# A streaming encoder kernel whose expert tiles are requested at another point of the program, with its gates read in six pieces

## The chip, the cores and the metric

The kernel runs on one core of a Trainium2 chip. The time is device microseconds of one execution, from the first to the last thing that the core does. Three executions of the kernel before took 3267.62, 3263.42 and 3265.85 us, a median of 3265.85 us. A separate execution was profiled.

## The reference

The program computes two residual layers and a final RMSNorm for 512 tokens of width 1024. A layer is a mixer (attention and pooling in the even layer, attention and a recurrence in the odd one) and then a PEER expert block, in which each token picks 8 x 16 of 16384 single-neuron experts. Only the expert block is touched by the change:

```python
def peer_ffn(h, w_query, sub_k1, sub_k2, expert_u, expert_v):
    q = (xt @ w_query).reshape(n_tok, PEER_HEADS, 2, PEER_DKEY // 2)
    s1 = jnp.einsum('thd,nd->thn', q[:, :, 0], sub_k1)
    s2 = jnp.einsum('thd,nd->thn', q[:, :, 1], sub_k2)
    v1, i1 = lax.top_k(s1, PEER_TOPK)
    v2, i2 = lax.top_k(s2, PEER_TOPK)
    ...
    top_s, pos = lax.top_k(cand.astype(jnp.float32), PEER_TOPK)
    idx = jnp.take_along_axis(cand_idx, pos, axis=-1)
    gate = jax.nn.softmax(top_s, axis=-1)
    ...
        u = expert_u[ib]
        act = jax.nn.gelu(jnp.einsum('thkd,td->thk', u, xb), approximate=False)
        ve = expert_v[ib]
        return jnp.einsum('thk,thkd->td', (gb * act).astype(ve.dtype), ve)
```

## The kernel before, in words

The expert block (function `peer`, called once per layer) splits the tokens. For the first 384 tokens it computes all 16384 experts densely, as 128 blocks of 128 experts: block j needs a u tile (512 KB), whose product with the tokens goes through a GELU and gives the activations of the block, and a v tile (512 KB), whose product with the activations times the gates is added up in six banks of PSUM. The last 128 tokens are done sparsely: 256 row fetches of 512 KB (`row`, issued by GpSimd, five buffers) are reduced by VectorE.

Every fp32 operand is split into a high and a low part and each product is three matmuls (`mm3`, lines 182 to 184, for u; line 1680 for v). ScalarE makes the high part (line 151), VectorE the low part (`ul` at line 1355, `vl` and `Hl` at line 176). A raw tile's buffer comes free when its low part is made.

The order of the work is the order of the code, engine by engine. Each engine runs its instructions in turn, and so does the queue of SyncE (SP), which issues nearly all loads: a DMA that has to wait for its buffer holds back all DMAs behind it on SP.

The dense part has these stages in each layer:

1. The u stage. Blocks 0 to 52 are multiplied by u (`u_step`), while VectorE works out which experts each token picked and makes the gates as one-hot products. The gates of 16 tokens at a time are written to DRAM by ScalarE's queue (`gd<-gs`, 1 MB each, 24 of them). Activations of blocks 0 to 12 stay in SBUF (`act`, NB_ACT = 13 buffers); those of blocks 13 to 52 (NB_SPILL = 40) are written to DRAM from a tile with two buffers (`acts`, `ad<-acts`).
2. The first 40 steps of the v loop. Step j splits v tile j + 1 (`v_load`), reads one spilled activation tile back (`a_load`), makes the gated activations of block j + 1 (`h_make`: `Hf`, `Hh`, `Hl`) and issues the 18 matmuls of block j (`v_mm`). From step 4 on VectorE also takes about 0.85 row per step (`g_work`).
3. Steps 40 to 114, in which each step also does the 24 matmuls of one of the 75 blocks left for u, and about 2.9 rows.
4. Steps 115 to 125 with v alone, the last two blocks token group by token group, and the output.

The gates of a group of 8 blocks are read back from DRAM as one DMA of 1536 KB in runs of 512 bytes (`g_load`, line 1633, tile `gt` with two buffers). A v tile (`vr`, three buffers) is requested in `v_fetch` (line 1642), called at the head of `v_load`; a u tile (`ur`, three buffers) in `u_fetch` (line 1340).

```python
            def v_load(j):
                if j < TAIL:
                    v_fetch(j + 1)
                g_load(j + 3)
                r = VR.pop(j)
...
            for j in range(TAIL):
                v_load(j + 1)
                if j < NB_SPILL:
                    a_load(NB_ACT + j)
                ...
                h_make(j + 1)
                v_mm(j)
```

Of the kernel before, what the change touches and what calls it, by code (L numbers as in the profile page):

```python
# [13 lines left out]
F32 = mybir.dt.float32  # L14
F32R = mybir.dt.float32r
# [10 lines left out]
P = 128  # L26
# [1266 lines left out]
TD = 384  # L1293
# [3 lines left out]
GB = 16  # L1297
GJ = 8
G_STEP = 4.2
NB_ACT = 13  # L1300
NB_SPILL = 40
ROWS = 5
# [5 lines left out]
def peer(k, layer):  # L1308
    nc, tc = k.nc, k.tc
    I = k.I  # L1310
    with ExitStack() as st:
# [30 lines left out]
        def u_load(j):  # L1342
            if j < NE:
                u_fetch(j)
                u_fetch(j + 1)
                r = U[j]
                h = up.tile([P, KD, P], F32R, name="uh", bufs=4)
                k.act(h, r, AF.Copy)
                U[j] = (h, r)
# [8 lines left out]
        def u_mm(j, spill=False):  # L1358
            h, l = U.pop(j)
            ps = psU.tile([P, T], F32, name="ups", tag="mm")  # L1360
            for d in range(KD):
                mm3(k, ps[:, :TD], (h[:, d, :], l[:, d, :]), (hh[:, d, :TD], hl[:, d, :TD]), d == 0, d == KD - 1)
            a = up.tile([P, TD], F32, name="acts") if spill else ap.tile([P, TD], F32, name="act")
            k.act(a, ps[:, :TD], AF.Gelu)
# [259 lines left out]
        with ExitStack() as st2:  # L1624
# [4 lines left out]

            def g_load(j):  # L1630
                if j < NE and j % GJ == 0:
                    g = vp.tile([P, TD // GB, GJ, GB], F32, name="gt")
                    nc.sync.dma_start(g, gd[:, :, j:j + GJ, :].rearrange("b p j t -> p b j t"))
                    GG[j // GJ] = g

            VR, fetched = {}, set()

            def v_fetch(j):
                if j < NE and j not in fetched:
                    fetched.add(j)  # L1640
                    VR[j] = vp.tile([P, D], F32, name="vr", bufs=3)
                    nc.sync.dma_start(VR[j], I["peer_vp"][layer, j])

            def v_load(j):
                if j < TAIL:
                    v_fetch(j + 1)
                g_load(j + 3)
                r = VR.pop(j)
# [3 lines left out]
                else:  # L1652
                    h = vp.tile([P, D], F32R, name="vh")
                    l = vp.tile([P, D], F32R, name="vl")
                split_act(k, h, l, r)
                VV[j] = (h, l)

            def h_make(j):
# [4 lines left out]
                if j == NE - 1:  # L1663

                    h, l = (up.tile([P, TD], F32R, name="acts") for _ in range(2))
                else:
# [121 lines left out]

            v_fetch(0)
            v_fetch(1)  # L1790
            g_load(0)
            v_load(0)
# [12 lines left out]
            for j in range(TAIL):  # L1805
# [9 lines left out]
                v_mm(j)  # L1815
                if j == TAIL - 5:
                    v_fetch(NE - 1)
                if j == TAIL - 4:
# [211 lines left out]
```

## Time and profile before

| | |
|---|---|
| median of three executions | 3265.85 us (3263.42 to 3267.62) |
| profiled execution | 3267.5 us |
| its span, first to last instruction | 3265.7 us (1.8 us lie around it) |
| TensorE busy | 3133.8 us, 96% of the span |
| VectorE busy | 2429.3 us, 74% |
| ScalarE busy | 1419.4 us, 43% |
| bytes moved by DMA | 792.67 MB, 243 GB/s on average |
| mean granted TensorE clock | 0.984 of full speed |

PE is TensorE's matmuls and PEld its weight loads, DVE is VectorE, ACT ScalarE, POOL GpSimd, SP SyncE; a q behind the name (SPq, ACTq) marks the engine's DMA issues. A matmul's duration in the trace includes time in which the next one already runs, so that a step's pace is read from the starts and not from the durations. A wait is put down to what came last. Times within the run are counted from the span's start. The u stage lies at about 405 to 675 us in layer 0 and 2105 to 2380 us in layer 1; the first 40 steps of the v loop run from 687 to 868 us and from 2389 to 2567 us.

### The profile page before, as it was taken

To read this page: it belongs to the slowest core of one execution; us is meant where nothing else is said; L and a number is where in the kernel's file an instruction comes from. 1 tells how busy PE (TensorE), PEld (TensorE's weight loads), DVE (VectorE), ACT (ScalarE), POOL (GpSimd) and SP (SyncE) were. 2 spreads that over 40 slices of the span, in tenths; PEclk is the share of its full clock that TensorE was granted. 3 is DMA by queue.
4 is the path that set the end of the run, shared out by engine and by line. 5 is a ranking of instruction groups with operands and counts; after the bars stand their busy time and mean duration, and the time that the engine had idled before them with its cause. 6 is when DMAs were issued, how large, how long until landed. Compare 5 with 4: busy or idle time off the path is not lost.

```text
span 3265.7 us, 55046 instructions
## 1 busy us (share of the span) xinstructions
PE 3133.8 (96%) x21696; PEld 2739.4 (84%) x21696; DVE 2429.3 (74%) x4725; ACT 1419.4 (43%) x1974; POOL 893.2 (27%) x696
## 2 busy tenths in 40 slices
PE   6998999999999999999999898999999999999998
PEld 5777899977799999997677787899977899999997
DVE  5246799957688888887666456899957788888886
ACT  3353367743333333333534534367733333333334
POOL 1004200023344444442220104100013344444442
PEclk8999999999999999999999999999999999999999
DMA  8523246799899999995621014256799999999984
GB/s 313 203 96 131 100 156 245 251 314 319 289 342 334 331 327 339 339 328 184 219 71 53 5 63 155 97 179 237 266 318 315 313 333 330 327 337 342 328 316 162
DMA packets 318276, 792.67 MB, mean 243 GB/s; under 512 B 23872, under 2 KB 159424, under 8 KB 305728
## 3 DMA queue, kind: packets, MB, share of 16 engines
q1 hardware_dynamic: 222992, 438.73, 38.8%
q0 software_dynamic: 75008, 274.78, 24.4%
q10 hardware_dynamic: 20016, 75.64, 6.1%
q8 instruction: 170, 2.79, 0.3%
q14 instruction: 90, 0.74, 0.1%
HBM read 714.57 MB, written 74.45 MB: 242 GB/s over the span
## 4 chain that ended last, share of the span: by engine, by line
PE 80%; DVE 9%; DMA 5%; ACT 4%; issue 3%; SPq 0%; ACTq 0%; DVEq 0%
PE o L1680 27%; PE ups L182 9%; PE ups L184 9%; PE ups L183 9%; PE bk L182 3%; PE bk L184 3%; PE bk L183 3%; DMA vr<-peer_vp 2%; PE bk L723 2%; PE qps L182 2%; PE gps L1568 2%; PE qps L183 2%; PE qps L184 2%; PE adaps L242 1%; DVE ul L1355 1%
## 5 line engine op out<-in xcount | busy, mean ns | idle before, releaser
L182 PE MATMUL ups<-phh,uh 128*128 128x384 f32 x2048 | 695.4, 340 | 6.6 <-ACT acts L151 6.6
L184 PE MATMUL ups<-phh,ul 128*128 128x384 f32 x2048 | 689.9, 337 | 0.0
L183 PE MATMUL ups<-phl,uh 128*128 128x384 f32 x2048 | 688.5, 336 | 0.0
L1702 POOL DMA_INDIRECT row<-peer_u,xres x256 | 344.5, 1346 | 1125.7 <-PE gps L1568 552.1
L151 ACT ACTIVATE vh<-vr 128x1024 fp32r<-128x1024 f32 x254 | 269.7, 1062 | 556.0 <-issue 454.0
L1680 PE MATMUL o<-vh,Hh 128*128 128x512 f32 x1524 | 477.9, 395 | 30.1 <-ACT Hh L151 30.1
L1680 PE MATMUL o<-vh,Hl 128*128 128x512 f32 x1524 | 474.5, 393 | 0.0
L1680 PE MATMUL o<-vl,Hh 128*128 128x512 f32 x1524 | 474.4, 393 | 0.0
L1702 POOL DMA_INDIRECT row<-peer_v,xres x256 | 337.4, 1318 | 428.2 <-DVE xres L1718 333.7
L176 DVE TENSOR_TENSOR vl<-vr,vh 128x1024 fp32r<-128x1024 f32 x254 | 311.0, 1224 | 131.4 <-ACT vh L151 129.9
L182 PEld LDWEIGHTS ups<-phh,uh 128*128 128x128 f32 x2048 | 387.1, 189 | 13.1 <-ACT acts L151 7.2
L183 PEld LDWEIGHTS ups<-phl,uh 128*128 128x128 f32 x2048 | 387.0, 189 | 5.8
L184 PEld LDWEIGHTS ups<-phh,ul 128*128 128x128 f32 x2048 | 386.5, 189 | 0.9 <-DVE ul L1355 0.6
L1680 PEld LDWEIGHTS o<-vh,Hh 128*128 128x128 f32 x1524 | 284.4, 189 | 86.6 <-ACT Hh L151 37.8
L1680 PEld LDWEIGHTS o<-vl,Hh 128*128 128x128 f32 x1524 | 288.2, 189 | 63.3
L1680 PEld LDWEIGHTS o<-vh,Hl 128*128 128x128 f32 x1524 | 288.0, 189 | 62.3
L1355 DVE TENSOR_TENSOR ul<-ur,uh 128x1024 fp32r<-128x1024 f32 x256 | 312.0, 1219 | 24.1 <-ACT uh L151 21.4
L1721 DVE SCALAR_TENSOR_TENSOR gacc<-row,xres,gacc 128x1024 f32<-128x1024 f32 x256 | 327.6, 1280 | 2.0 <-DMA row<-peer_v,xres 1.2
L176 DVE TENSOR_TENSOR Hl<-Hf,Hh 128x384 fp32r<-128x384 f32 x254 | 141.9, 559 | 241.4 <-ACT Hh L151 241.4
L1718 DVE SCALAR_TENSOR_TENSOR xres<-row,xres 128x1024 f32<-128x1024 f32 x256 | 311.8, 1218 | 0.6 <-DMA row<-peer_u,xres 0.6
L151 ACT ACTIVATE uh<-ur 128x1024 fp32r<-128x1024 f32 x256 | 269.6, 1053 | 22.3 <-DMA ur<-peer_uT 7.2
L151 ACT ACTIVATE act<-ups 128x384 f32<-128x384 f32 x176 | 86.5, 492 | 370.6 <-PE ups L184 370.5
(475 smaller groups left out, 4583.7 us busy)
## 6 DMA issues: line engine op xcount, KB each, us to landing
ur<-peer_uT SPq DMA_DIRECT2D x256, 512.0 KB, 5.8
vr<-peer_vp SPq DMA_DIRECT2D x256, 512.0 KB, 7.0
gt<-gd SPq DMA_DIRECT2D x32, 1536.0 KB, 15.5
adaw<-ada_w SPq DMA_DIRECT2D x32, 1024.0 KB, 7.0
wraw<-peer_wq SPq DMA_DIRECT2D x32, 512.0 KB, 3.4
ad<-acts ACTq DMA_DIRECT2D x80, 192.0 KB, 3.6
act<-ad SPq DMA_DIRECT2D x80, 192.0 KB, 5.0
wraw<-od_w_in SPq DMA_DIRECT2D x30, 512.0 KB, 3.6
```

The lines of the kernel that those rows point to most:

```text
L151: return self.nc.scalar.activation(out, in_, func, **kw)
L176: (eng or k.nc.vector).tensor_tensor(lo, src, hi.bitcast(F32), op=ALU.subtract)
L182: mm(out, w[0], x[0], start=start, stop=False, skip_group_check=True)
L183: mm(out, w[0], x[1], start=False, stop=False, skip_group_check=True)
L184: mm(out, w[1], x[0], start=False, stop=stop, skip_group_check=True)
L723: mm(ps[h, a, :], l(h, a), r(h, a), start=start and a == 0, stop=stop, skip_group_check=True)
L1355: nc.vector.tensor_tensor(l, r, h.bitcast(F32), op=ALU.subtract)
L1568: nc.tensor.matmul(ps[:, i, :], A[:, 2 * q + i // 2, :, i % 2], B[r][:, 2 * q + i // 2, :, i % 2], start=r == 0, stop=r == 1, skip_group_c ...
L1680: mm(O_[t][b], w[:, ts], v[:, 512 * b:512 * b + 512], start=s, stop=e, skip_group_check=True)
L1702: nc.gpsimd.indirect_dma_start(out=r, out_offset=None, in_=I[f"peer_{kind}{layer}"], in_offset=bass.IndirectOffsetOnAxis(ap=eidx[:, c:c + ...
L1718: nc.vector.scalar_tensor_tensor(junk, r, 1.0, htok, op0=ALU.mult, op1=ALU.mult, accum_out=dots[:, c:c + 1])
L1721: nc.vector.scalar_tensor_tensor(acc, r, wts[:, c:c + 1], acc, op0=ALU.mult, op1=ALU.add)
```

## The change

One activation buffer of 13 becomes a third buffer of the spilled activations, so that 12 blocks stay in SBUF and 41 are spilled; the sum of 53 is unchanged. `v_fetch` is called behind the split of a v tile and requests the tile that will take the buffer which that split frees, three blocks ahead; the order of the requests is a list, in which the last block's tile stands where it is used. `u_load` requests up to two blocks ahead in place of one. The gates of a group of 8 blocks are read by six DMAs of 256 KB (four blocks of 16 tokens each), one in each of the first six steps of the group before; the first group is still one DMA.

```diff
--- before.py
+++ after.py
@@ -1297,8 +1297,8 @@
 GB = 16
 GJ = 8
 G_STEP = 4.2
-NB_ACT = 13
-NB_SPILL = 40
+NB_ACT = 12
+NB_SPILL = 41
 ROWS = 5
 ADA_M = 12
 TAIL = NE - 2
@@ -1341,8 +1341,8 @@
 
         def u_load(j):
             if j < NE:
-                u_fetch(j)
-                u_fetch(j + 1)
+                for i in range(3):
+                    u_fetch(j + i)
                 r = U[j]
                 h = up.tile([P, KD, P], F32R, name="uh", bufs=4)
                 k.act(h, r, AF.Copy)
@@ -1360,7 +1360,7 @@
             ps = psU.tile([P, T], F32, name="ups", tag="mm")
             for d in range(KD):
                 mm3(k, ps[:, :TD], (h[:, d, :], l[:, d, :]), (hh[:, d, :TD], hl[:, d, :TD]), d == 0, d == KD - 1)
-            a = up.tile([P, TD], F32, name="acts") if spill else ap.tile([P, TD], F32, name="act")
+            a = up.tile([P, TD], F32, name="acts", bufs=3) if spill else ap.tile([P, TD], F32, name="act")
             k.act(a, ps[:, :TD], AF.Gelu)
             if spill:
                 nc.scalar.dma_start(ad[j - NB_ACT], a)
@@ -1627,24 +1627,28 @@
             O_ = [[psO.tile([P, 512], F32, name=f"o{t}{b}") for b in range(2)] for t in range(NTD)]
             VV, GG, HH = {}, {}, {}
 
-            def g_load(j):
-                if j < NE and j % GJ == 0:
-                    g = vp.tile([P, TD // GB, GJ, GB], F32, name="gt")
-                    nc.sync.dma_start(g, gd[:, :, j:j + GJ, :].rearrange("b p j t -> p b j t"))
-                    GG[j // GJ] = g
-
-            VR, fetched = {}, set()
-
-            def v_fetch(j):
-                if j < NE and j not in fetched:
-                    fetched.add(j)
+            def g_load(j, parts):
+
+                if j >= NE:
+                    return
+                if j // GJ not in GG:
+                    GG[j // GJ] = vp.tile([P, TD // GB, GJ, GB], F32, name="gt")
+                b = slice(4 * parts[0], 4 * parts[-1] + 4)
+                nc.sync.dma_start(GG[j // GJ][:, b], gd[b, :, j:j + GJ, :].rearrange("b p j t -> p b j t"))
+
+            VR = {}
+
+            order = list(range(TAIL - 2)) + [NE - 1] + list(range(TAIL - 2, NE - 1))
+
+            def v_fetch():
+                if order:
+                    j = order.pop(0)
                     VR[j] = vp.tile([P, D], F32, name="vr", bufs=3)
                     nc.sync.dma_start(VR[j], I["peer_vp"][layer, j])
 
             def v_load(j):
-                if j < TAIL:
-                    v_fetch(j + 1)
-                g_load(j + 3)
+                if j < TAIL and j % GJ < 6:
+                    g_load(j // GJ * GJ + GJ, [j % GJ])
                 r = VR.pop(j)
                 if j == NE - 1:
                     h, l = (up.tile([P, KD, P], F32R, name=nm, bufs=b).rearrange("p a b -> p (a b)")
@@ -1653,6 +1657,7 @@
                     h = vp.tile([P, D], F32R, name="vh")
                     l = vp.tile([P, D], F32R, name="vl")
                 split_act(k, h, l, r)
+                v_fetch()
                 VV[j] = (h, l)
 
             def h_make(j):
@@ -1662,7 +1667,7 @@
                                         ACTS.pop(j).rearrange("p (b t) -> p b t", t=GB), g[:, :, j % GJ, :], op=ALU.mult)
                 if j == NE - 1:
 
-                    h, l = (up.tile([P, TD], F32R, name="acts") for _ in range(2))
+                    h, l = (up.tile([P, TD], F32R, name="acts", bufs=3) for _ in range(2))
                 else:
                     h = vp.tile([P, TD], F32R, name="Hh")
                     l = vp.tile([P, TD], F32R, name="Hl")
@@ -1786,9 +1791,9 @@
                 nc.vector.tensor_scalar(o[:, 512:], ps[1], k.r[:, t:t + 1], None, op0=ALU.mult)
                 nc.sync.dma_start(k.O["out_0_dram"][t * P:t * P + P, :], o)
 
-            v_fetch(0)
-            v_fetch(1)
-            g_load(0)
+            for _ in range(3):
+                v_fetch()
+            g_load(0, range(6))
             v_load(0)
             while ju < NB_ACT + NB_SPILL:
                 if ju == NB_ACT + NB_SPILL - 1:
@@ -1813,8 +1818,6 @@
                     ju += 1
                 h_make(j + 1)
                 v_mm(j)
-                if j == TAIL - 5:
-                    v_fetch(NE - 1)
                 if j == TAIL - 4:
                     v_load(NE - 1)
                 if j == TAIL - 3:
```

The order of SP's DMAs where the v loop of layer 0 begins, before. `ur` are u tiles, `vr` v tiles, `gt` the gates of a group of 8 blocks, `act` a spilled activation tile read back:

```order
L1340 DMA ur_7478<-peer_uT 128x1024
L1642 DMA vr_7527<-peer_vp 128x1024
L1642 DMA vr_7529<-peer_vp 128x1024
L1633 DMA gt_7531<-gd_2790 128x24x128
L1340 DMA ur_7539<-peer_uT 128x1024
L1340 DMA ur_7579<-peer_uT 128x1024
L1642 DMA vr_7617<-peer_vp 128x1024
L1372 DMA act_7623<-ad_2791 128x384
```

The same place after the change:

```order
L1340 DMA ur_7481<-peer_uT 128x1024
L1647 DMA vr_7530<-peer_vp 128x1024
L1647 DMA vr_7532<-peer_vp 128x1024
L1647 DMA vr_7534<-peer_vp 128x1024
L1637 DMA gt_7536<-gd_2790 128x24x128
L1637 DMA gt_7538<-gd_2790 128x4x128
L1647 DMA vr_7544<-peer_vp 128x1024
L1340 DMA ur_7548<-peer_uT 128x1024
L1340 DMA ur_7588<-peer_uT 128x1024
L1637 DMA gt_7538<-gd_2790 128x4x128
```

One v tile more stands in front of the first gates, and one u tile fewer between them and the fourth v tile: the u tile that stood just behind the gates is now the one in front of the first v tile (the u requests are one block ahead of where they were).

SP's order inside the first 40 steps, at the read of the second group's gates, before, with the semaphores that each DMA waits for (DVE is VectorE, Activation ScalarE, Pool GpSimd, DMAHW0 to 7 those of earlier DMAs):

```order
L1372 DMA act_7719<-ad_2791 128x384 [waits DVE_49]
L1642 DMA vr_7745<-peer_vp 128x1024 [waits DMAHW6_49,DMAHW0_49,Activation_49]
L1633 DMA gt_7747<-gd_2790 128x24x128 [waits DMAHW7_49,Pool_49]
L1372 DMA act_7753<-ad_2791 128x384 [waits DVE_49]
L1642 DMA vr_7782<-peer_vp 128x1024 [waits DMAHW2_49,DMAHW1_49,Activation_49]
```

After, at the end of one group's pieces and the start of the next:

```order
L1637 DMA gt_7538<-gd_2790 128x4x128 [waits DMAHW7_49]
L1647 DMA vr_7763<-peer_vp 128x1024 [waits DMAHW0_49,DVE_49]
L1372 DMA act_7765<-ad_2791 128x384 [waits DMAHW1_49]
L1647 DMA vr_7798<-peer_vp 128x1024 [waits DMAHW2_49,DVE_49]
L1372 DMA act_7800<-ad_2791 128x384 [waits DMAHW3_49]
L1647 DMA vr_7833<-peer_vp 128x1024 [waits DMAHW5_49,DMAHW4_49,DVE_49]
L1372 DMA act_7835<-ad_2791 128x384
L1637 DMA gt_7864<-gd_2790 128x4x128 [waits DMAHW6_49,DVE_49]
```

The wait for VectorE has moved from the activation tile to the v tile, which now stands in front of it; the read of 24 x 128 has become reads of 4 x 128, each with a v tile behind it.

## Rows read from the trace of the kernel before

**Rows 1.** The page's first part: busy time of each engine, share of the span, instructions.

```profile
PE 3133.8 (96%) x21696; PEld 2739.4 (84%) x21696; DVE 2429.3 (74%) x4725; ACT 1419.4 (43%) x1974; POOL 893.2 (27%) x696
```

**Rows 2.** Busy time by stretch: stretch in us, its length, then PE, PEld, DVE, ACT and POOL busy with instructions in brackets, granted clock, busy share of the 16 DMA engines, GB/s.

```profile
450.00:500.00 50.00, 50.00 (x396) 48.59 (x395) 49.55 (x84) 38.70 (x45) 0.00 (x0) 1.00 0.63 219
655.00:687.00 32.00, 24.72 (x152) 24.02 (x150) 8.48 (x10) 14.05 (x18) 5.83 (x5) 0.95 1.01 357
728.00:769.00 41.00, 39.41 (x174) 32.26 (x174) 29.86 (x45) 15.20 (x20) 12.46 (x8) 1.00 0.95 328
769.00:810.00 41.00, 39.55 (x175) 32.39 (x174) 31.60 (x48) 14.97 (x21) 14.95 (x9) 1.00 0.94 309
810.00:868.00 58.00, 51.10 (x207) 41.34 (x206) 36.88 (x49) 18.04 (x24) 14.78 (x11) 0.91 0.88 301
868.00:1478.00 610.00, 610.00 (x3089) 555.71 (x3088) 498.42 (x615) 213.92 (x299) 274.34 (x214) 1.00 0.94 331
950.00:1000.00 50.00, 50.00 (x254) 45.50 (x254) 41.56 (x53) 17.59 (x25) 22.64 (x19) 1.00 0.99 353
2518.00:2567.00 49.00, 44.24 (x181) 35.69 (x180) 32.33 (x44) 15.79 (x21) 12.70 (x9) 0.93 0.91 311
```

**Rows 3.** TensorE's waits for the gated activations, in us in total, times and the longest, in three stretches in this order: 687 to 868 us, 2395 to 2567 us, and 868 to 1560 us.

```profile
PE o L1680 <- ACT Hh L151: 13.6, 5, 3.7
PE o L1680 <- ACT Hh L151: 9.2, 5, 2.6
PE o L1680 <- ACT Hh L151: 2.2, 3, 0.8
```

**Rows 4.** From the chain of waits (start, us, what): a v tile's transfer in the chain, and the 18 matmuls of the last step without u in layer 0 and in layer 1.

```profile
741.40 6.80 DMA vr<-peer_vp
...
861.60 5.99 PE o L1680 x18
...
2560.78 5.99 PE o L1680 x18
```

**Rows 5.** SP's timeline around one read of gates: start, us of the issue, what.

```profile
733.10 0.39 SPq L1642 DMA_DIRECT2D vr<-peer_vp  x1
733.54 0.48 SPq L1633 DMA_DIRECT2D gt<-gd  x1
736.77 4.53 SPq L1372 DMA_DIRECT2D act<-ad  x1
741.40 0.37 SPq L1642 DMA_DIRECT2D vr<-peer_vp  x1
```

**Rows 6.** VectorE's timeline (first two) and ScalarE's (last two): a v tile's low part and the gated activations behind it, and two of the v tiles' high parts, six steps apart.

```profile
730.97 1.23 DVE L176 TENSOR_TENSOR vl<-vr,vh 128x1024 fp32r<-128x1024 f32 x1
732.11 0.55 DVE L1661 TENSOR_TENSOR Hf<-act,gt 128x384 f32<-128x384 f32 x1
...
709.47 1.06 ACT L151 ACTIVATE vh<-vr 128x1024 fp32r<-128x1024 f32 x1 [0.67 <-PE o L1680]
...
733.95 1.06 ACT L151 ACTIVATE vh<-vr 128x1024 fp32r<-128x1024 f32 x1 [0.67 <-PE o L1680]
```

**Rows 7.** The page's list of DMA issues: count, KB each, median us from issue to landing.

```profile
vr<-peer_vp SPq DMA_DIRECT2D x256, 512.0 KB, 7.0
gt<-gd SPq DMA_DIRECT2D x32, 1536.0 KB, 15.5
...
act<-ad SPq DMA_DIRECT2D x80, 192.0 KB, 5.0
```

**Rows 8.** The start of the v loop. First from the chain of waits in layer 0: the last write of gates and the first read of them. Then TensorE's timeline, with the idle time before an instruction in square brackets: the last u block before the loop and the first v block in layer 0, the first and the second v block in layer 1.

```profile
662.12 11.68 DMA gd<-gs__7250
673.87 12.01 DMA gt<-gd
...
677.40 0.45 PE L182 MATMUL ups<-phh,uh 128*128 128x384 f32 x1 [2.98 <-ACT acts L151]
687.07 0.73 PE L1680 MATMUL o<-vh,Hh 128*128 128x512 f32 x2 [3.65 <-ACT Hh L151]
...
2389.23 0.73 PE L1680 MATMUL o<-vh,Hh 128*128 128x512 f32 x2 [2.93 <-ACT Hh L151]
...
2395.01 0.73 PE L1680 MATMUL o<-vh,Hh 128*128 128x512 f32 x2 [1.42 <-ACT Hh L151]
```

**Rows 9.** Timelines at the same place in layer 0: SP's issues, then VectorE's low part of a u tile, then the ScalarE instruction that waits for a spill buffer.

```profile
665.27 1.32 SPq L1642 DMA_DIRECT2D vr<-peer_vp  x2
673.87 0.38 SPq L1633 DMA_DIRECT2D gt<-gd  x1
676.83 5.40 SPq L1340 DMA_DIRECT2D ur<-peer_uT  x2
...
666.19 1.23 DVE L1355 TENSOR_TENSOR ul<-ur,uh 128x1024 fp32r<-128x1024 f32 x1 [1.33 <-PE ups L184]
...
676.86 0.49 ACT L151 ACTIVATE acts<-ups 128x384 f32<-128x384 f32 x1 [8.71 <-DMA ad<-acts]
```

**Rows 10.** DMA queues from 657 to 690 us: packets, MB, and the time of the packets as a share of the 16 engines' time. q1 is SP's queue, q10 ScalarE's.

```profile
q1 hardware_dynamic: 4432, 6.11, 54.7%
...
q10 hardware_dynamic: 908, 2.95, 22.2%
```

## The prediction, made before the changed kernel had run

> **What bounds the kernel now.** I began with the page's first part: TensorE is busy for 96% of the span [rows 1], so that an edit pays only where TensorE stands still or runs at a lower clock. To find those places I read the busy time by stretch. In the u stage VectorE has 49.55 of 50 us in work and the DMA engines are at 0.63, so an earlier transfer can give nothing there. From 868 to 1478 us TensorE fills 610 of 610 us at the full clock; nothing can be won there either. In the first 40 steps of the v loop TensorE has 39.41 and 39.55 of 41 us and 51.10 of 58 us, and the granted clock falls to 0.91, in layer 1 to 0.93 [rows 2]. So two stretches of some 180 us matter.
>
> Next came the pace. ScalarE's splits of v tiles start at 709.47 and, six steps later, at 733.95 us [rows 6]: 4.08 us a step when nothing is late. Forty steps would take 163.2 us. In layer 0 they run from 687.07 [rows 8] to 861.60 + 5.99 = 867.59 us [rows 4], 180.5 us, 17.3 too long; in layer 1 from 2389.23 to 2560.78 + 5.99 = 2566.77 us, 177.5 us, 14.3 too long.
>
> TensorE's waits say where it goes. They are 13.6 us in layer 0, of which 3.65 is the wait before the first step [rows 3, 8], so 9.95 within the stage; in layer 1 they are 9.2 us. The rest is the clock: 0.09 x 58 = 5.2 us in the last stretch of layer 0 and 0.07 x 49 = 3.4 us in that of layer 1, where TensorE comes out of a wait at the lower of its two levels, 1.2 instead of 2.4 GHz [rows 2]. Together 9.95 + 5.2 + 9.2 + 3.4 = 27.7 us that belong to late data.
>
> The chain and SP's timeline show which data. A read of gates is issued at 733.54 us; the activation read behind it then holds SP's queue for 4.53 us, and so the next v tile, for which SP was ready at about 737, is asked for at 741.40 and lands 6.80 us later [rows 4, 5]. A v tile must come within two steps or TensorE stands. The median landing of a gates read is 15.5 us, that of a v tile 7.0 [rows 7]. So the bound in this stage is a burst in one in-order queue, once in eight steps.
>
> **Gates in six pieces.** The bytes stay the same, and so does the length of a run. Per group five DMAs are added; at about 0.4 us an issue [rows 5] that is 2 us of SP in 32.6 us, and SP mostly waits. What goes is the block of 1536 KB ahead of a v tile; a v tile now has 256 KB in front of it. The price of the stage at best is the whole 27.7 us. At worst it is nothing: if the DMA engines have no more to give, the waits are only spread. From 728 to 810 us they were 0.95 and 0.94 busy while TensorE missed 1.59 + 1.45 = 3.04 of 82 us; the same work in 79 us needs a share of 0.945 x 82 / 79 = 0.98. The stretch from 950 to 1000 us shows 0.99 with TensorE at 50 of 50 us [rows 2], so 0.98 can be carried. I take it that one wait of 2 us per layer is left, or several small ones, and count 27.7 - 4 = 23.7 us.
>
> **The v request behind the split.** The buffer of tile m is free when the low part of tile m - 3 is made; that is so in both kernels. Before, the request stood behind an activation read that waits for `Hf`, which VectorE makes next after the low part. It ended at 732.11 + 0.55 us, and the request went out at 733.10; the low part was done at 730.97 + 1.23 = 732.20 [rows 5, 6]. So the request moves forward by about 0.9 us, from 9.0 to 9.9 us ahead of its use two steps behind the split at 733.95. Alone that does not close a wait of up to 2.6 us; I count it inside the term above. The activation read loses its wait, since with 12 buffers it takes one that is free a step earlier, and it is needed 11 steps later: nothing.
>
> **The u request.** The wait for the low part three blocks back is the same event as before, so in the u stage and from step 41 on the requests leave at the same moments. Cost and gain are nothing, with VectorE at 49.55 of 50 us as cover in the u stage; without it a u tile would be worth at most its place in the queue. In the query projection one u request now waits for the first low part ahead of the last weight tile; that tile then waits some 3 us in SP's queue and is used more than 15 us later.
>
> **The start of the loop.** Here the change costs. TensorE's first v block waits for the gates: last write 662.12 + 11.68, read 673.87 + 12.01 us [rows 8]. Before, two v tiles stood in front of that read, and a u tile behind it went out at 676.83. Now this u tile and three v tiles stand in front, so 1 MB more lies ahead in a queue that is full: the DMA engines are at 1.01 and move 357 GB/s [rows 2]. If SP's queue gets all of that, the gates come 1.05 MB / 357 GB/s = 2.9 us later; if it keeps its share of 54.7% [rows 10], 5.4 us; if the tiles have drained by then, 0. I take 2.9 in each layer, 5.8 us. The first v request also moves back, from 665.27 to about 667.5, behind a low part made at 666.19 + 1.23 us [rows 9]; that stays in the shadow of the gates.
>
> The gates' own write goes through ScalarE's queue, whose packets had 22.2% of the engines' time beside SP's 54.7% [rows 10]. The Trainium skill says that each DMA engine takes turns between the queues that have work, packet by packet (DMA: Bandwidth & Descriptors, "Queues, rings and completion order"). By that a longer line on SP leaves the write where it is; with one line for all it would come 2.9 us later too, and the start would cost 11.6 us in place of 5.8. The rows fit the rule, but do not single it out.
>
> **The third spill buffer.** ScalarE's wait of 8.71 us for a spill buffer goes [rows 9], and with it TensorE's 2.98 us before the last u block. What is late next is the first v block, which waits for the gates and not for that block: 3.65 us of waiting become about 6.6 plus the shift above. I count nothing; if the gates came earlier, up to 2.98 us a layer would be won. The one spill more, 192 KB out and in, lies under VectorE's work, and one more step with a read stands against one fewer of the last steps, both at 4.08 us. The last block's tile is requested in order instead of late: TensorE waits 2.2 us after step 40 [rows 3], none of it for a DMA: nothing.
>
> **Sum.** 23.7 - 5.8 = 17.9 us. The profiled execution takes 3267.5 us with a span of 3265.7, and would take 3249.6; the median of the runs lies 1.65 us lower, so I forecast 3248 us. Its own range, from no waits left and a free start to 4 us left in each layer and 5.4 at each start, is 3238 to 3257.
>
> **Rivals.** (a) All waits go, and the first read is not delayed: 3265.85 - 27.7 = 3238 us. For it: 353 GB/s with no wait; against it: the full queue at 655 us. (b) The stage is short of bandwidth. In layer 0 the stretches with waits move 309 to 328 GB/s at 0.94 and 0.95; if runs of 512 bytes are what costs, spreading them leaves half the waits: 13.9 - 5.8 = 8 us, 3258. (c) The change does not do what it says: the waits come from the bytes of a group and not from their standing in one line, and only the start is felt: 3266 to 3272. Against it, SP's 4.53 us and the fact that waits follow the reads. (d) Slower: three buffers for v close a loop. A tile is asked for at a low part, lands after T, gets its high part (1.06 us) and its low part (1.23), and this must fit three steps: T up to 12.24 - 2.3 = 9.9 us. Now a read of gates stands before nearly every v tile; if each then took the 11.68 us of the write [rows 8], a step would take (11.68 + 2.3) / 3 = 4.66 us and 41 steps 191 us, against 180.5 + 4.1 and 177.5 + 4.1 now: 6.4 + 9.4 + 5.8 = 21.6 us slower, 3287. It decides from T = 11 us, where the stages are as long as now. Against it: v tiles land in 7.0 us at the median.
>
> Activation reads of 192 KB land in 5.0 us and v tiles of 512 KB in 7.0 [rows 7], two in each step of 4.08 us, so transfers overlap. The Trainium skill asks for 1 MiB or more per DMA for bandwidth and gives some 2 us of fixed time to each (DMA: Bandwidth & Descriptors, "Rules for kernel authors" and "Anatomy of one DMA — SWDGE"). By that five DMAs more a group would be 10 us of fixed time; as an estimate from that page, served one by one over five groups, 50 us a layer. The rows speak against one by one.
>
> **Chances.** Forecast 0.55, (a) 0.14, (b) 0.17, (c) 0.06, (d) 0.08. The bound of 0.2% is 6.5 us, about what runs of this kernel can tell from no change: faster is below 3259.3, slower above 3272.4. Forecast, (a) and two thirds of (b) make faster 0.80; the rest of (b) and most of (c) same 0.11; (d) and the end of (c) slower 0.09. The range from 3234 to 3264 us holds the forecast, (a) and nearly all of (b).
>
> **What would show it.** In the changed profile TensorE's waits for `Hh` in the first 41 steps should be under 4 us a layer, the clock there 1.00 behind the first ten us, no issue on SP longer than about 1 us behind a gates piece, and v tiles landing within 9 us. The first gates read should land about 2.9 us later than 685.9, with the spill wait gone. The u stage and the steps with u should keep their times. The forecast is wrong if the waits are merely spread, if v tiles take over 10 us, or if the start is late by more than 5 us.

## The result, and the profile after

The changed kernel took 3247.76 us (median of six executions, 3245.79 to 3252.01) beside 3267.41 us for the kernel before on the same chip (six, 3263.42 to 3273.45): a ratio of 0.9938, with a 95% interval from 0.9928 to 0.9948. The forecast was 3248.0 us. The profiled execution took 3248.3 us with a span of 3246.5, which is 19.2 us less than the one profiled before.

The first part of the page of the changed kernel:

```profile
PE 3126.6 (96%) x21696; PEld 2737.1 (84%) x21696; DVE 2429.1 (75%) x4725; ACT 1420.4 (44%) x1974; POOL 904.6 (28%) x696
```

TensorE has 7.2 us less in work for the same 21696 matmuls [rows 1], which fits fewer of them at the lower clock (below, the granted clock of each stretch). Busy time by stretch of the changed kernel (stretch, length, PE, PEld, DVE, ACT, POOL, granted clock, DMA share, GB/s):

```profile
450.00:500.00 50.00, 50.00 (x399) 48.58 (x398) 49.55 (x84) 39.18 (x44) 0.00 (x0) 1.00 0.63 225
...
728.00:769.00 41.00, 41.00 (x183) 33.95 (x182) 31.88 (x48) 15.89 (x20) 14.41 (x8) 1.00 1.01 356
769.00:810.00 41.00, 41.00 (x183) 33.96 (x182) 33.05 (x51) 16.04 (x22) 16.12 (x9) 1.00 0.97 337
810.00:858.00 48.00, 48.00 (x214) 39.75 (x213) 37.96 (x50) 18.77 (x24) 17.76 (x10) 1.00 0.97 332
858.00:1478.00 620.00, 620.00 (x3138) 564.83 (x3137) 505.95 (x623) 216.54 (x304) 279.98 (x217) 1.00 0.94 332
2503.00:2552.00 49.00, 49.00 (x218) 40.59 (x217) 38.66 (x52) 19.07 (x24) 17.75 (x10) 1.00 0.96 334
```

Where TensorE missed time inside the two stages before [rows 2], it now fills every stretch shown at the full clock; the DMA engines carry 0.96 to 1.01 there, against 0.88 to 0.95. The u stage and the steps with u are as they were.

The chain of waits of the changed kernel, from the last write of gates to the end of the first 41 steps, and the one row of layer 1 that answers to that stage:

```profile
661.82 0.33 ACTq L1572
...
663.72 11.59 DMA ad<-acts
675.37 12.59 DMA gt<-gd
...
689.15 169.69 PE o L1685 x738
...
2382.89 169.35 PE o L1685 x738
```

In each layer 738 matmuls, the 41 steps of 18, stand in one row: nothing interrupted TensorE. That is 167.3 us at 4.08 a step and some 2.3 us more at the lower clock behind the first wait. SP's timeline of the changed kernel shows a step inside the stage and then the start (start, us of the issue, what):

```profile
706.23 0.33 SPq L1647 DMA_DIRECT2D vr<-peer_vp  x1
706.61 0.43 SPq L1372 DMA_DIRECT2D act<-ad  x1
707.08 0.43 SPq L1637 DMA_DIRECT2D gt<-gd  x1
```
```profile
667.48 5.17 SPq L1647 DMA_DIRECT2D vr<-peer_vp  x3
675.37 8.62 SPq L1637 DMA_DIRECT2D gt<-gd  x2
```

The issue of 4.53 us behind a read of gates [rows 5] is gone; this step's three DMAs each take under half a microsecond to issue (in layer 1 three of the pieces take 1.0 to 1.6 us). On the page the landings of the changed kernel's DMAs are (count, KB each, median us):

```profile
vr<-peer_vp SPq DMA_DIRECT2D x256, 512.0 KB, 6.6
gt<-gd SPq DMA_DIRECT2D x180, 256.0 KB, 7.8
...
act<-ad SPq DMA_DIRECT2D x82, 192.0 KB, 6.6
```

What is left is one wait at each start, by TensorE's timeline in both layers:

```profile
689.15 1.22 PE L1685 MATMUL o<-vh,Hh 128*128 128x512 f32 x2 [10.91 <-ACT Hh L151]
...
2382.89 1.22 PE L1685 MATMUL o<-vh,Hh 128*128 128x512 f32 x2 [10.56 <-ACT Hh L151]
```

**Where the 19.2 us come from.** I time each layer from the issue of the last gates write, at 661.82 and 2354.93 us (before: 662.12 and 2364.46). From there to the first v block it took 24.95 and 24.77 us before and takes 27.33 and 27.96: 2.4 and 3.2 us lost. From there to the first u block among the v steps, with 41 steps on both sides (before has 40 there, so I add the 4.08 us of one), it took 867.59 + 4.08 - 687.07 = 184.6 and 2566.77 + 4.08 - 2389.23 = 181.6 us, and takes 169.7 and 169.35: 14.9 and 12.3 us won. That makes 27.2 - 5.6 = 21.6 us. The layers' tails give 1.2 and 0.6 us more. Some 4.4 us go again between the end of layer 0's steps and 2355 us, 2.0 of them ahead of layer 1's u stage and 2.4 in it. This same part takes 816.8 to 821.3 us in the thirteen profiled executions of this document, 817.0 to 821.3 with the u requests of the change and 816.8 to 819.7 without. So most of the 4.4 us is what this part varies by from one execution to the next; why it varies is not shown.

### The profile page after: what moved, and what is told of

Same layout as the page of the kernel before. It is cut to its first block, busy times and chain, and to the rows that moved or that the text cites. A ratio compares the mean times of both kernels' runs of the same rounds, so it can differ in the third digit from the quotient of the medians.

```text
span 3246.5 us, 55223 instructions
## 1 busy us (share of the span) xinstructions
PE 3126.6 (96%) x21696; PEld 2737.1 (84%) x21696; DVE 2429.1 (75%) x4725; ACT 1420.4 (44%) x1974; POOL 904.6 (28%) x696
## 4 chain that ended last, share of the span: by engine, by line
PE 85%; DVE 7%; ACT 3%; DMA 3%; issue 2%; POOL 0%; ACTq 0%; DVEq 0%; SPq 0%
PE o L1685 31%; PE ups L182 9%; PE ups L184 9%; PE ups L183 9%; PE bk L182 3%; PE bk L184 3%; PE bk L183 3%; PE bk L723 2%; PE gps L1568 2%; PE qps L182 2%; PE qps L184 2%; PE qps L183 2%; PE adaps L242 1%; PE sps L1422 1%; DVE ul L1355 1%
## 5 line engine op out<-in xcount | busy, mean ns | idle before, releaser
L1707 POOL DMA_INDIRECT row<-peer_v,xres x256 | 345.0, 1348 | 428.1 <-DVE xres L1723 344.6
L1685 PEld LDWEIGHTS o<-vh,Hh 128*128 128x128 f32 x1524 | 284.0, 188 | 76.1 <-ACT Hh L151 27.3
L1355 DVE TENSOR_TENSOR ul<-ur,uh 128x1024 fp32r<-128x1024 f32 x256 | 312.0, 1219 | 25.9 <-ACT uh L151 22.2
L151 ACT ACTIVATE uh<-ur 128x1024 fp32r<-128x1024 f32 x256 | 269.7, 1054 | 22.2 <-DMA ur<-peer_uT 7.7
```

What stands on the lines that cost most here:

```text
L151: return self.nc.scalar.activation(out, in_, func, **kw)
L1355: nc.vector.tensor_tensor(l, r, h.bitcast(F32), op=ALU.subtract)
L1685: mm(O_[t][b], w[:, ts], v[:, 512 * b:512 * b + 512], start=s, stop=e, skip_group_check=True)
L1707: nc.gpsimd.indirect_dma_start(out=r, out_offset=None, in_=I[f"peer_{kind}{layer}"], in_offset=bass.IndirectOffsetOnAxis(ap=eidx[:, c:c + ...
```

## The experiments

My theory A: the burst of 1536 KB in one in-order queue makes the waits, and the pieces take them away; the moved request alone does little. Rivals: the request's place does it (B), both are needed (C). For the late start, theory D: the first gates read is not held by the bytes ahead of it but by a semaphore; rivals: by those bytes after all (E), or the DMA engines are full, and the order of the requests decides nothing (F). The first four experiments, the next four and the last three ran on three chips, each beside the kernel before (medians 3266.61, 3268.77 and 3270.12 us); between these groups I compare ratios.

**The pieces alone.** The kernel before with this edit:

```diff
-            def g_load(j):
-                if j < NE and j % GJ == 0:
...
+            def g_load(j, parts):
...
-                g_load(j + 3)
+                if j < TAIL and j % GJ < 6:
+                    g_load(j // GJ * GJ + GJ, [j % GJ])
```

> The kernel before with one edit: each group of gates but the first is read in six pieces, one per step; the requests of v and u tiles stay where they were, and the spill keeps two buffers. Theory A (the burst of 1536 KB in SP's one queue makes the v tiles late): the waits inside the first 40 steps go, from 9.95 and 9.2 us to under 3 us a layer, and the start of the loop keeps its old form, so about 25 us faster than before, 3242 us, or even a little faster than the changed kernel. Rival B (the place of the request is what counts: a v tile stood behind an activation read that holds the queue): the waits stay at 7 us or more a layer and the time within 6 us of before. Rival C (both halves are needed): in between, 8 to 14 us faster.

Measured: 3245.11 us (3244.02 to 3245.91), ratio 0.9935 [0.9922, 0.9948], level with the whole change. Its chain in layer 0 still holds one v tile; layer 1's stage, here 40 steps, is whole:

```profile
727.07 10.39 DMA vr<-peer_vp
...
2378.58 165.82 PE o L1684 x720
```

The pieces alone do it, as A said: TensorE's one wait inside the two stages is 0.95 us.

**The moved requests alone.** The changed kernel with a group's gates as one DMA at the old place:

```diff
-                if j < TAIL and j % GJ < 6:
-                    g_load(j // GJ * GJ + GJ, [j % GJ])
+                g_load(j + 3)
```

> The changed kernel with the gates of a group read by one DMA again, issued where the kernel before issues it. Theory A: the four late v tiles per layer are back with 2 to 4 us each, and the start costs what it costs in the changed kernel (about 2.4 us a layer), so 3265 to 3272 us. Rival B: the waits stay away, 3245 to 3251 us. Rival C: about 3257 us.

Measured: 3252.8 us (3248.99 to 3263.69), ratio 0.9963 [0.995, 0.9976]. A missed this: by A the requests were worth nothing, and they are worth some 12 to 14 us, together with the third spill buffer and the earlier u requests, which this kernel has too. SP's timeline, TensorE's waits inside the two stages (690 to 868, then 2390 to 2567 us) and a stretch of it:

```profile
737.89 0.43 SPq L1633 DMA_DIRECT2D gt<-gd  x1
741.07 4.23 SPq L1644 DMA_DIRECT2D vr<-peer_vp  x1
745.34 0.43 SPq L1372 DMA_DIRECT2D act<-ad  x1
```
```profile
PE o L1681 <- ACT Hh L151: 3.5, 4, 1.5
...
PE o L1681 <- ACT Hh L151: 3.6, 2, 2.0
```
```profile
810.00:868.00 58.00, 56.38 (x253) 46.54 (x252) 43.86 (x58) 21.75 (x28) 17.38 (x11) 1.00 0.94 331
```

The long issue is still there, now on the v tile itself, and a v tile is still late after nearly every read of gates: ScalarE waits for one five times in layer 0 and four times in layer 1, 8.6 and 8.3 us, where it waited 14.8 and 12.5 us, four times each, before. But the waits are 3.5 and 3.6 us where they were 9.95 and 9.2, none longer than 2.0, and the clock stays at 1.00 where it fell to 0.91. 12.05 us of waits and the 8.6 us of clock, less the 2.2 and 3.1 us that its two starts lose, make 15.4; its profiled execution is 16.5 us shorter than that of before. So each half alone takes most of the same waits, and the gains overlap: 22 and 14 us alone, 20 with both.

**One v tile fewer in front of the gates.** The changed kernel with the third v request behind the first read of gates:

```diff
-            for _ in range(3):
-                v_fetch()
+            v_fetch()
+            v_fetch()
             g_load(0, range(6))
+            v_fetch()
```

> The changed kernel with the third v request of the start put behind the first read of gates instead of in front of it. In the changed kernel that read is issued at 675.37 us, 3.1 us after the last write of gates has landed (661.82 + 10.5), because it waits for the semaphore of a spill write. Theory D (that semaphore is what costs the start): the read now gets the semaphore of the last write of gates, is issued at about 672.3 us, and the loop starts some 3 us earlier in each layer: 3242 us. Rival E (the bytes in front of the read cost the start): the issue stays near 675 us, the read takes 1 to 1.5 us less for the 512 KB fewer in front of it: 3245 us. Rival F (neither; the DMA engines are full until 688 us and whatever is read first, the first product comes then): no change, 3248 us.

Measured: 3244.04 us (3242.17 to 3251.14), ratio 0.9938 [0.9925, 0.995]. Theory D rests on the order of SP's DMAs, whose eight semaphores (DMAHW0 to 7, shared with ScalarE's DMAs) go round: a DMA waits for the last one that used its semaphore, whatever that was. In the changed kernel:

```order
L1647 DMA vr_7534<-peer_vp 128x1024 [waits DMAHW3_49]
L1637 DMA gt_7536<-gd_2790 128x24x128 [waits DMAHW4_49,PE_49]
```

and the waits of SP in the profile of the changed kernel from 655 to 700 us:

```profile
SPq L1637 <- DMA ad<-acts: 5.0, 2, 2.7
...
SPq L1647 <- DMA gd<-gs__7253: 3.8, 1, 3.8
```

The write of the last gates landed at 661.82 + 10.5 us = 672.3, and released the third v tile. The read behind it waited for the next semaphore, that of a spilled activation tile which it does not read, until 675.37: 3.1 us. With two v tiles in front, the read takes the gates' own semaphore and goes when they land. The chain of this experiment, in layer 0 and layer 1:

```profile
673.06 11.95 DMA gt<-gd
...
2349.99 10.39 DMA gd<-gs__23716
2360.44 14.45 DMA gt<-gd
```

In layer 1 the read leaves 10.45 us after the write was issued, in the changed kernel 2368.80 - 2354.93 = 13.87 us after; the start comes at 25.3 and 26.1 us instead of 27.3 and 28.0. So D is right on the time of the issue. The gain in time is not resolved: the two starts come 3.9 us earlier together and the median is 3.7 us lower, but the ratio is that of the whole change (0.9938), the executions spread over 9 us, and in layer 1 the read itself took 14.45 us instead of 12.90, which the runs do not explain.

**Two spill buffers.** The changed kernel with 13 and 40 blocks and two buffers again:

```diff
-NB_ACT = 12
-NB_SPILL = 41
+NB_ACT = 13
+NB_SPILL = 40
```

> The changed kernel with 13 activation buffers, 40 spilled blocks and two spill buffers again. If the third buffer gives nothing, as forecast: ScalarE's wait of about 9 us for a spill buffer and TensorE's of about 3 us before the last u block are back, the wait for the first gates is about 7 instead of 10.9 us, and the time is that of the changed kernel, 3248 us within 3. Rival: the spill wait delays the split of the first v and u tiles, and the loop starts 2 to 3 us later in each layer: 3252 to 3254 us.

Measured: 3251.0 us (3248.19 to 3251.78), ratio 0.9952 [0.994, 0.9965]. Its stages are unbroken too; TensorE waits 9.7 and 6.2 us before the first v blocks. These come 27.6 and 27.7 us after the last gates write was issued, with three buffers 27.3 and 28.0, although ScalarE waits 6.9 us for a spill buffer again in layer 0: the start does not feel the third buffer. The time leaves some 3 us open, since the interval meets that of the whole change.

**Six pieces at once.** The changed kernel with the six reads issued back to back in one step, so that only their spreading is lost:

```diff
-                if j < TAIL and j % GJ < 6:
-                    g_load(j // GJ * GJ + GJ, [j % GJ])
+                if j + 3 < NE and (j + 3) % GJ == 0:
+                    for p in range(6):
+                        g_load(j + 3, [p])
```

> The changed kernel with all six pieces of a group issued one behind the other in one step, where the kernel before issues its one read. The number of DMAs and their size stay, the burst is back. If the burst is what makes v tiles late: waits as in the run with one read per group and the requests moved (some 10 us over both layers beside the two starts), 3250 to 3256 us. If smaller DMAs as such help (a v tile is served between them): 3246 to 3249 us, no waits inside the stage.

Measured: 3251.83 us (3249.21 to 3255.34), ratio 0.9947 [0.9932, 0.9961]. Late v tiles are back in part. SP's timeline and the chain, both in layer 0, then TensorE's waits inside the two stages (700 to 868 us, then 2392 to 2567) and a stretch:

```profile
808.14 5.59 SPq L1637 DMA_DIRECT2D gt<-gd  x6
```
```profile
813.83 8.35 DMA vr<-peer_vp
```
```profile
PE o L1686 <- ACT Hh L151: 2.3, 2, 1.8
...
PE o L1686 <- ACT Hh L151: 0.3, 1, 0.3
```
```profile
810.00:868.00 58.00, 55.66 (x240) 45.41 (x239) 42.16 (x58) 20.88 (x28) 18.47 (x12) 0.97 0.95 328
```

SP is held for 5.59 us in front of the v tile that then stands in the chain. But in the profiled execution, the slowest of the five, the time is that of the first expectation and the waits, 2.3 and 0.3 us, are nearly those of the second, and the ratio's interval meets that of the whole change (0.9928 to 0.9948) as well as that of one DMA per group (0.995 to 0.9976). So a burst of pieces can still make a v tile late; how much of the gain lies in spreading the pieces and how much in their size is not resolved.

**Gates on ScalarE's queue.** The kernel before with the gates from the second group on issued by ScalarE, so that SP's line is free of them:

```diff
-                    nc.sync.dma_start(g, gd[:
+                    (nc.scalar if j else nc.sync).dma_start(g, gd[:
```

> The kernel before with one edit: the gates of all groups but the first are read by the same single DMA of 1536 KB, issued on ScalarE's queue instead of SP's. The bytes still come in one burst, but no v tile stands behind them in a queue and SP is not held. If the in-order queue is the cause: the waits of 9.95 and 9.2 us go to under 4 us a layer, 3240 to 3247 us. If the burst takes the bandwidth whatever its queue: the waits stay, 3262 to 3270 us. In between (the engines take turns, a v tile gets half the rate): 3250 to 3258 us.

Measured: 3292.55 us (3282.12 to 3299.52), ratio 1.0063 [1.0045, 1.0081]: slower, which none of the theories expected. The DMAs of this experiment from 690 to 868 us, queues (packets, MB, share) and landings:

```profile
q1 hardware_dynamic: 10423, 26.05, 39.6%
q0 software_dynamic: 4089, 15.18, 25.7%
q10 hardware_dynamic: 14491, 7.42, 15.2%
...
vr<-peer_vp SPq DMA_DIRECT2D x38, 512.0 KB, 6.6
gt<-gd ACTq DMA_DIRECT2D x5, 1536.0 KB, 21.7
```

and the same read in the kernel before, same stretch:

```profile
gt<-gd SPq DMA_DIRECT2D x5, 1536.0 KB, 11.6
```

No issue on SP is long any more (none above 0.7 us in this stretch). But the gates land after 21.7 us, where the kernel leaves them three steps, 12.2 us, and TensorE waits for them 17.5 us in this stage. In SP's line the 3072 short runs went through in 11.6 us while what stood behind them waited; in a line of their own, beside two others that go on, they had 15.2% of the engines' time over this stretch. The Trainium skill says that spreading DMAs over several issuing engines does not help, since all run on the same 16 DMA engines (DMA: Bandwidth & Descriptors, "Rules for kernel authors"); here it nearly doubled the landing of one of them. The pieces have more time: they are asked for three to eight steps before they are used.

This run also tells the line from the bytes. ScalarE's waits for v tiles from 690 to 868 us, in the kernel before and here:

```profile
ACT vh L151 <- DMA vr<-peer_vp: 14.8, 4, 4.9
...
ACT vh L151 <- DMA vr<-peer_vp: 3.2, 2, 2.2
```

The gates still come in one burst, but out of SP's line they hardly make a v tile late, and no v tile stands in the chain of either stage. One reserve: while TensorE waits for gates, each v tile has more time to land.

**Row fetches held.** The experiment with two v tiles in front, and in it the first five row fetches kept back by a copy on GpSimd until the first v tile's low part is made:

```diff
+            nc.gpsimd.tensor_copy(dots[:, P - 1:P], VV[0][1][:, 0:1].bitcast(F32))
             g_fetch(3)
```

> The kernel with two v tiles in front of the first gates (3244.04 us), and the first five row fetches of GpSimd (2.6 MB, issued from 658 to 664 us, wanted from step 4 on) held back until the first v tile has been split, by a copy on GpSimd that reads its low part. If the start of the loop is bound by the DMA engines, which are full from 655 to 688 us, 2.6 MB / 357 GB/s = 7.3 us of transfers are out of the way: last write and first read of gates land earlier, the loop starts 4 to 7 us earlier in each layer, 3230 to 3236 us. If it is bound by the order in SP's queue alone: no change, 3244 us. If the rows then come into the first steps and make v tiles late: 3242 to 3250 us.

Measured: 3232.87 us (3230.94 to 3234.57), ratio 0.9888 [0.9872, 0.9904]: the fastest of all. GpSimd's timeline, and then rows of the DMAs from 655 to 692 us, without the hold (the experiment with two in front) and with it: a queue's share and the landing of the last gates write:

```profile
678.65 1.11 POOL L1804 COPY xres<-vl 128x1 f32<-128x1 f32 x1 [294.73 <-DVE vl L176]
679.94 1.16 POOL L1707 DMA_INDIRECT row<-peer_u,xres  x1 [0.17 <-POOL xres L1804]
```
```profile
q0 software_dynamic: 720, 2.62, 20.6%
...
gd<-gs__7253 ACTq DMA_DIRECT2D x1, 1024.0 KB, 12.1
```
```profile
gd<-gs__7253 ACTq DMA_DIRECT2D x1, 1024.0 KB, 5.9
```

The fetches, which went out from about 658 us on, now go 20 us later; the write of gates lands in 5.9 us instead of 12.1 and the first v block starts 21.4 us after the issue of that write (684.28 - 662.93) instead of 25.3, in layer 1 22.2 us instead of 26.1. So the first half of F holds: the start is bound by DMA engines, of whose time the row fetches (q0, GpSimd's queue) took 20.6% without the hold.

**First gates cut five and one.** The changed kernel with one v tile and five sixths of the first gates in front, the last sixth and two v tiles behind:

```diff
-            for _ in range(3):
-                v_fetch()
-            g_load(0, range(6))
+            v_fetch()
+            g_load(0, range(5))
+            g_load(0, [5])
+            v_fetch()
+            v_fetch()
```

> The changed kernel with the first group's gates read by two DMAs, one of 1280 KB that does not need the last four writes of gates and one of 256 KB that does, both between the first and the second v tile. Against two v tiles in front and one read (3244.04 us): the large part is on its way some 4 us before the last write lands, so the loop starts 2 to 4 us earlier in each layer, 3236 to 3241 us, if the wait for the last write is what counts; if the engines are simply full until 685 us, as good as no change, 3242 to 3245 us.

Measured: 3242.72 us (3240.24 to 3244.37), ratio 0.9918 [0.9904, 0.9932]. Against two in front (3244.04 us, ratio 0.9938, on another chip) the intervals meet; the first v blocks come 24.9 and 25.2 us after the last gates write was issued instead of 25.3 and 26.1. So the bytes' order in a full queue matters little here.

**The hold in the other kernels.** The same copy in the kernel before, in that with the pieces alone, and in the changed one with three v tiles in front:

```diff
+            nc.gpsimd.tensor_copy(dots[:, P - 1:P], VV[0][1][:, 0:1].bitcast(F32))
             g_fetch(3)
```

> The kernel before with the first five row fetches held until the first v tile's low part is made, and nothing else changed. If the first steps of the loop are bound by DMA engines that the row fetches share, both starts of this kernel too come 4 to 6 us earlier and the waits inside the stage stay: 3256 to 3260 us beside 3267 for the kernel before. If the gain seen with the rows held needs the other edits (a stage already without waits), the time stays at 3264 to 3270.

Measured: 3255.3 us (3248.61 to 3257.14), ratio 0.995 [0.9936, 0.9963]. The hold needs none of the other edits. The first v blocks come 18.8 and 19.8 us after the last gates write was issued, earlier than with the hold and the changed requests (21.4 and 22.2), and the waits inside the stages stay, 9.7 and 10.3 us.

> The kernel before with the gates in six pieces and the first five row fetches held; requests, buffers and order of the v tiles as before. If the moved requests and the third spill buffer add nothing once the gates are in pieces and the start is free, 3231 to 3236 us, level with 3232.9 for the version that has all of them. If the moved requests still carry part of it, 3238 us or more, with waits for v tiles inside the first 40 steps.

Measured: 3245.56 us (3238.86 to 3248.51), ratio 0.9924 [0.9911, 0.9938]. Five executions spread over 10 us, and the profiled one (3238.86) is the fastest of them. Its first v blocks come 17.8 and 18.3 us after the gates write was issued, and from 690 and 2390 us on it waits 1.0 us and not at all. But the second v block waits in both layers. ScalarE's timeline in layer 0, then TensorE's in both:

```profile
683.92 1.06 ACT L151 ACTIVATE uh<-ur 128x1024 fp32r<-128x1024 f32 x1 [2.82 <-DMA ur<-peer_uT]
...
689.15 0.73 PE L1684 MATMUL o<-vh,Hh 128*128 128x512 f32 x2 [3.65 <-ACT Hh L151]
...
2376.99 1.22 PE L1684 MATMUL o<-vh,Hh 128*128 128x512 f32 x2 [2.80 <-ACT Hh L151]
```

ScalarE makes the high part of a u tile ahead of that of the second v tile, and the u tile is late; in layer 1 the chain has a u tile at the same place. So the time is that of the second expectation, but what is late is a u tile at the head and not v tiles inside. With the changed requests and the hold there is no such wait. Whether the earlier u request or the third spill buffer removes it, and what the slower executions wait for, stays open.

> The changed kernel (three v tiles in front of the first gates read) with the first five row fetches held. If the first gates read is held by the landing of a spill write with which it shares a semaphore, that is still so, but the write lands sooner with the engines less full: 3235 to 3240 us, 2 to 6 us above the 3232.9 of the version with two tiles in front. If the full engines alone made the start late, the number of tiles in front does not matter: 3231 to 3234.

Measured: 3235.74 us (3232.59 to 3240.78), ratio 0.9896 [0.9881, 0.9911]: where D put it, but its interval meets that of two in front, so that the semaphore's price with the rows held is not resolved by the time. In the traces the first gates read leaves 7.7 and 7.2 us after the write was issued, with two in front and the hold 6.7 and 6.8: little of the 3.1 us is left.

## Why the prediction was right, and where its steps were not

**What bounds the kernel.** Right: the burst in SP's line. In pieces spread over six steps the late v tiles go (the pieces alone), and with the gates out of that line most go too, although the burst stays (gates on ScalarE's queue). The pieces put back together bring some of them back (six at once).

**Gates in six pieces.** Right in kind, a little low in size: I counted 27.7 - 4 = 23.7 us, and 27.2 came. The 4 us that I held back for leftover waits were not needed. The engines carried 0.97 to 1.01 in layer 0 where I had worked out 0.98, so that rival (b) falls; rival (d) falls with v tiles landing in 6.6 us.

**The v request behind the split.** This is the step that failed: "Alone that does not close a wait of up to 2.6 us; I count it inside the term above". It closes none, and that half was right, but TensorE's waits come out at 2.0 us at most, 7.1 us in all where they were 19.15, and in that trace the clock does not fall again behind the start. Alone the requests, with the third buffer, are worth 12 to 14 us; that a request 0.9 us earlier is the reason is not shown. In the sum this did no harm, since the pieces take the same waits away.

**The start.** I put 2.9 us in each layer, for 1 MB more in a full queue. 2.4 and 3.2 us were lost, but the cause was another, so this step failed too. In layer 0 the read took 12.59 us against 12.01 [rows 8], 0.6 us more, and the rest is its later issue, 13.55 us behind that of the write against 11.75. The write itself landed 1.2 us sooner than before (10.5 against 11.68; in layer 1 10.8 both times); the wait of 3.1 us for a spill write's semaphore ate this and 1.8 us more. The size was right by luck. The rule from the Trainium skill that I weighed (DMA: Bandwidth & Descriptors, "Queues, rings and completion order") is not at odds with this: the write on the other queue took 10.5 us, not 2.9 us longer than 11.68. But it was hardly put to the test, since beside the write stood only one u tile more: the third v tile left at 672.32 us, when the write had landed.

**Third buffer, u requests, tail.** The wait of 8.71 us for a spill buffer [rows 9] is gone, and ScalarE waits for a v tile in its place, in its timeline of the changed kernel:

```profile
678.92 1.06 ACT L151 ACTIVATE vh<-vr 128x1024 fp32r<-128x1024 f32 x1 [8.48 <-DMA vr<-peer_vp]
```

TensorE's last u block does not wait any more, and the first v block waits 10.91 us instead of 2.98 + 3.65; nothing was won, as I said. The u stage has the same 49.55 us of VectorE. The tails gave 1.2 and 0.6 us, where I had counted nothing.

**Six DMAs for one.** The Trainium skill's advice of 1 MiB or more per DMA (DMA: Bandwidth & Descriptors, "Rules for kernel authors") spoke against the pieces. Measured, six of 256 KB for one of 1536 KB, one a step, were worth 22 us here (the pieces alone). No run here shows the fixed time for each DMA that the prediction's estimate of 50 us a layer rests on: with five DMAs more a group each stage got 12 to 15 us shorter.

**The sum.** 23.7 - 5.8 = 17.9 against 27.2 - 5.6 = 21.6 in the places that I named, and 19.2 in the whole execution; the 2.4 us between are the 4.4 us that went ahead of and in layer 1's u stage, less the tails.

That the forecast lies 0.24 us from the median is luck: 3.7 us more came in the places that I named, 2.4 went again elsewhere, and the median of the kernel before rose from 3265.85 us (three executions) to 3267.41 (six).

## What to carry to other kernels

In an in-order queue a large read with short runs cost what stood behind it: cut it and spread the pieces over the steps before it is needed, rather than move it to a queue of its own, where it may land far later. Where DMA engines are full at the head of a loop, look for transfers in other queues that are not needed yet; holding five row fetches back won more than any order of the requests there. Before moving a DMA by one place, look at which earlier DMA lends it its semaphore.

## What the runs showed of the hardware

- Waits can cost more than their length, by the clock: in the kernel before, with waits up to 3.7 us, the granted clock was 0.91 over 58 us, part of them at the lower level (1.2 GHz). The length of a wait alone does not tell: with the moved requests alone, waits of up to 2.0 us left it at 1.00 (2.4 GHz), and with six pieces at once, waits of up to 1.8 us came with 0.97 over the same 58 us.
- The same read of 3072 short runs landed in 11.6 us on SP's queue and in 21.7 us on ScalarE's.
- A write of 1 MB landed in 5.3 and 5.9 us (two layers) with no row fetches beside it and in 9.8 to 12.1 us with five, in the runs whose landings are recorded.
- A DMA of this program waits for the last one that used its semaphore, of eight; at the start of the changed kernel that cost 3.1 us for a tile that it does not read.
- The issue behind a read of 3072 short runs on SP took 3.0 to 4.5 us inside the two stages of the kernel before; beside it stand issues of 0.4 to 0.5.
